# A fixed order for three engines in the scan and attention stage, and the scan's output in five parts

## The chip, the core and the metric

The kernel runs on one core of a Trainium2 chip. The metric is the time of one execution in microseconds (us), lower is better. A core has TensorE (PE, matrix products), VectorE (DVE), ScalarE (ACT) and GpSimd (POOL) for work on whole tiles, and SyncE (SP), which here only issues DMA transfers. Each engine takes its own list of instructions and waits on semaphores where it needs another engine's result or a free buffer. TensorE reads SBUF and writes PSUM, which has eight banks.

## The reference

One encoder layer over a prompt of 256 tokens and a sample of 2048 tokens, 2304 rows of 1024 in all, with float32 accuracy. A normalised input is projected once; the columns split into an RWKV-7 group (eight heads of 64, scanned forward and backward) and an attention group (eight query heads, two key heads). What the change touches:

```python
# scan, for each head, in both directions
S = S * w_t + sa * b_t + v_t * k_t          # 64 x 64 state
y_t = S r_t
y = y_f + y_b
yn = (y - mean(y)) * rsqrt(var(y) + 64e-5)  # over the 64 of a head
out_rwkv = (yn * lnx_w + lnx_b + bonus) * g
# attention, blocks of 128 queries
p = softmax(q k^T / 8);  out_att = p v
```

Both outputs are joined, projected, and followed by a gated feed-forward block.

## The kernel before

The work runs in stages: input projection with the preparation of the scan's operands (`e_phase`) to about 865 us; the start of attention beside the end of that preparation and the first two triangular inversions, to about 1015 us; scan and attention side by side, to about 2425 us; output projection and feed-forward for three groups of 768 rows, to the end.

**Interleaving.** Scan, attention and inversions are Python generators. `beside` runs the scan and for each of its yields calls attention `RATE_S` times the yielded weight (3.45 calls for a weight of 1). One call of attention emits one unit. In the scan's `rest(k)` each element also calls the inversions (`back`) once; it has eight elements in steps 0 to 3 and five in the others, and a step has four rests.

**Scan** (`scan`, `scan_chain`). 36 steps; step `k` takes one 64-token chunk forward and one backward. A step has three dependent parts on TensorE with copies on ScalarE between them (lines 720 to 731), the state update on VectorE (734, 736), and the output sum (742, 745). The Gram matmuls of the next step (`scan_gram`, line 664) and the transposes (`scan_turn`) use PSUM tiles `g`, of which there are two. In the first visit to a chunk its output goes to DRAM (`yd`), in the second it is read back (`y2`) and added (`yt`, line 762). When both chunks of a 128-token tile are done, `scan_out` centres and scales it (lines 780 to 788, with a mean and a power on POOL), transposes it into a `g` tile, multiplies by `g` from DRAM (`yg`, line 805), adds `bg` (`ybg`) on POOL (line 807) and stores it from `yo`. `yo`, `yg` and `ybg` have one buffer each. Tiles become complete in pairs, at every second step of the second half.

**Attention** (`att_scores`, `att_values`). For each group of four heads and each tile of 128 queries there are 16 units (four for a prompt tile): a unit is one head against 512 keys. Scores take two matmuls (lines 934, 935: keys in a high and a low part) into PSUM tile `as` (two banks); VectorE takes the row maximum (938); ScalarE the exponential `p` with its sum (939). After the last unit the factors `f` follow, and POOL multiplies all 16 `p` tiles by them (956). The values run behind, in halves, two per unit: one half transposes four `p` blocks into `at` (968) and splits them into a high part on ScalarE (`pth`, line 177) and a low part on VectorE (`ptl`, line 183); the next half multiplies both with the values (979). `ATT_LAG` sets how many units the values lie behind.

**Order.** A planner orders the instructions of each engine by estimated times and by priority, which goes by the source's order; `high_priority(offset=AHEAD)` moves the maximum, the exponential and the split forward. In the scan and the rest of attention `manual_schedule` fixes TensorE to the order of the source; VectorE, ScalarE, POOL and SP are planned. Outside this stage all are planned.

**Inversions** (`inv_block`). Ten blocks, (group, direction), in a fixed order, four of them (`INV_POOL`) on POOL: load, 31 steps of two operations (lines 570, 572), a transposed copy, stores and loads, a wait of 16 calls, then up to four rounds of matmuls, a masked product (604) and a copy. `load(k + 2)` in the scan calls `back` without a pause until the blocks that the step needs are ready.

The functions that the change touches:

Of the kernel before, what the change touches and what calls it, by code (L numbers as in the profile page):

```python
# [12 lines left out]
ALU = mybir.AluOpType  # L13
# [30 lines left out]
AHEAD = 300  # L44
ATT_LAG = 2
RATE_E, RATE_S = 1.0, 3.45
PB, XB, W_BUFS = 22, 2, 4
# [51 lines left out]
class Kern:  # L99
# [441 lines left out]
    def inv_block(self, bi, d, sb, eng):  # L541
# [25 lines left out]
        yield  # L567
# [7 lines left out]
        nc.vector.tensor_copy(out=xt, in_=xs.rearrange(tr))  # L575
# [18 lines left out]
        for _ in range(16):  # L594
            yield
# [106 lines left out]
    def scan_chain(self, step, nxt, sb, ps):  # L702
# [25 lines left out]
        act.copy(out=sg[0:64, :, 1, :], in_=hb[64:128].rearrange(f))  # L728
        yield
# [14 lines left out]
        for d, q, e, rows in heads:  # L744
            nc.tensor.matmul(psy[rows, d, q, :], mrb[:, d, q, e, :], sav[0:64, d, q, e, :], start=False, stop=d + q == 4,
                             skip_group_check=True)
        if nxt is not None:
            self.scan_sv(nxt, st, sb)
# [5 lines left out]
        else:  # L754
            for d, c in enumerate(step["c"]):
                y2 = T("y2", [P, 4, C], 2)
                self.ld(y2, self.yd[c])
# [4 lines left out]
                dve.tensor_tensor(out=yt[:, c % 2], in0=psy[:, d], in1=y2, op=ALU.add)  # L762
                self.ydone[tile] = self.ydone.get(tile, 0) + 1
                if self.ydone[tile] == 2:
                    self.outs.append(self.scan_out(tile, yt, sb, ps))
                    next(self.outs[-1])
        yield

    def scan_out(self, tile, y, sb, ps):
# [18 lines left out]
        dve.tensor_tensor(out=hv, in0=hv, in1=bc(r), op=ALU.mult)  # L788
        yield
# [4 lines left out]

        g = T("yg", [P, 2, 2, P], 1)
        bg = T("ybg", [P, 2, 2, P], 1)
        yo = T("yo", [P, 2, 2, P], 1)
        half = lambda t, q: t[q % 2 * 64:q % 2 * 64 + 64, q // 2]
        dr = lambda t, t0=t0: t.rearrange("(e c) t -> c e t", e=2)[:, :, t0:t0 + P]
        for q in range(4):  # L800
            self.ld(half(g, q), dr(self.gdr[q]))
            self.ld(half(bg, q), dr(self.bgd[q]))
# [8 lines left out]
    def scan(self, back, sb, ps):  # L811
# [31 lines left out]
        for k, step in enumerate(steps):  # L843
            last = k + 1 == len(steps)
            chain = self.scan_chain(step, None if last or steps[k + 1]["st"] is not step["st"] else steps[k + 1], sb, ps)
            for d in range(2):
# [3 lines left out]
                for i, r in enumerate(rest(k)):  # L850
                    if d == 0 and i == 2:

                        for g in self.outs:
                            next(g, None)
                        self.outs = []
                    yield r
            next(chain)
            yield from rest(k)
# [4 lines left out]
        for g in self.outs:  # L863
            next(g, None)


    def att_kv(self, g, sb, ps):
# [5 lines left out]
        def load(b):  # L873
            if b < len(KBLOCKS):
# [4 lines left out]
                for i in range(2):  # L879
                    self.lda(kd[:, :w, i, :], self.kd[t0:t1, gs].rearrange("(j p) c -> p j c", p=P))  # L880
                self.lda(vr, self.vd[t0:t1, gs].rearrange("(j p) c -> p j c", p=P))
# [18 lines left out]
    def att_q(self, g, t0, sb, ps):  # L900
# [3 lines left out]
        for i in range(2):  # L904
            self.lda(qd[:, :, i, :], self.qd[t0:t0 + P, g * 256:(g + 1) * 256].rearrange("p (h c) -> p h c", c=64))
# [10 lines left out]
    def att_scores(self, qs, t0, kv, sb, ps):  # L916
# [13 lines left out]
        for i in range(nh):  # L930
            kh, kl = kv[parts[i]][:2]
            for h in range(4):
                pss = ps.tile([P, 512], F32, name="as", tag="as", bufs=2)
                nc.tensor.matmul(pss[:, :hw], qs[:, h, :], kh, start=True, stop=False)  # L934
                nc.tensor.matmul(pss[:, :hw], qs[:, h, :], kl, start=False, stop=True)  # L935
                p_ = S("p", [P, 512], PB)
                with self.tc.high_priority(offset=AHEAD):
                    dve.tensor_reduce(out=nm[:, h, i:i + 1], in_=pss[:, :hw], axis=AX.X, op=ALU.max, negate=True)  # L938
                    act.activation(out=p_[:, :hw], in_=pss[:, :hw], func=AF.Exp, bias=nm[:, h, i:i + 1],  # L939
                                   accum_out=ls[:, h, i:i + 1])  # L940
                pt[h, i] = p_
                yield
# [555 lines left out]
```

## Time and profile before

| | |
|---|---|
| time, median of 3 runs | 4222.75 us (4220.28 to 4224.4) |
| the profiled execution | 4225.85 us, span of its instructions 4224.1 us |
| busy, share of the span | PE 91%, DVE 67%, ACT 48%, POOL 32% |
| chain that ended last | PE 65%, DVE 15%, POOL 6%, issue 5%, DMA 4%, ACT 3% |
| mean granted TensorE clock | 0.953 of 2.4 GHz |

The profile is one execution. Engines are busy while they execute; matmuls are pipelined and their ends are modelled, so a busy PE is not PE at its peak. PEld is TensorE's loading of the stationary operand, SPq and ACTq are the DMA issues of an engine. A row `A <- B: us, times` says how long engine and line A sat idle until B released it.

### The profile page before, as it was taken

How to read it: one execution, taken by the hardware profiler on the slowest of the kernel's cores; microseconds unless marked ns; L12 is line 12 of the kernel's file. 1: busy time of each engine (PE TensorE's matmuls, PEld its weight loads, DVE VectorE, ACT ScalarE, POOL GpSimd, SP SyncE). 2: the span in 40 equal slices, each digit the busy share in tenths (PEclk: the TensorE clock that was granted, in tenths of full speed). 3: DMA queues.
4: the chain of work that ended last, by engine and by line, in shares of the span. 5: the costliest groups of instructions: out<-in, count | busy, mean ns of one | idle time of the engine just before them, and what ended most of it. 6: DMA issues, size and time to landing. Idle time of an engine off the chain costs nothing.

```text
span 4224.1 us, 70455 instructions
## 1 busy us (share of the span) xinstructions
PE 3846.1 (91%) x26208; PEld 3306.5 (78%) x26208; DVE 2828.8 (67%) x4337; ACT 2041.3 (48%) x3922; POOL 1351.2 (32%) x1882
## 2 busy tenths in 40 slices
PE   8999999878888887887888879999989999989998
PEld 7988878656666665666666669998879998889987
DVE  5477686899776866667776657764477754477743
ACT  5344444456655564556565634443344443344432
POOL 2244353634636362734344312210122210122200
PEclk9999999789989998989999989999999999999999
DMA  6576576652443335333332252324523343423241
GB/s 201 164 211 211 182 207 199 195 137 43 108 90 85 78 75 120 88 80 92 88 90 72 62 181 83 102 95 175 175 93 99 104 171 109 165 88 107 100 170 70
DMA packets 646871, 524.27 MB, mean 124 GB/s; under 512 B 368512, under 2 KB 555520, under 8 KB 646528
## 3 DMA queue, kind: packets, MB, share of 16 engines
q1 hardware_dynamic: 576944, 438.23, 35.0%
q0 software_dynamic: 16944, 68.43, 4.9%
q10 hardware_dynamic: 52640, 13.11, 1.4%
q8 instruction: 206, 3.38, 0.3%
q14 instruction: 137, 1.12, 0.1%
HBM read 355.59 MB, written 166.37 MB: 124 GB/s over the span
## 4 chain that ended last, share of the span: by engine, by line
PE 65%; DVE 15%; POOL 6%; issue 5%; DMA 4%; ACT 3%; SPq 2%; ACTq 0%; DVEq 0%; POOLq 0%
PE acc L1171 22%; PE acc L213 8%; PE acc L214 8%; PE acc L215 8%; PE ao L979 3%; PE at L968 3%; DVE nm L938 3%; DVE ptl L183 2%; PE g L664 2%; PE as L934 2%; DVE cl L668 1%; PE as L935 1%; POOL p L956 1%; SPq L112 1%; DVE i L570 1%
## 5 line engine op out<-in xcount | busy, mean ns | idle before, releaser
L1171 PE MATMUL acc<-H,wsh 128*128 128x384 f32 x3168 | 813.7, 337 | 32.2 <-ACT cg L1199 22.6
L1171 PEld LDWEIGHTS acc<-H,wsh 128*128 128x128 f32 x3168 | 577.6, 190 | 35.8 <-ACT cg L1199 23.8
L1171 PE MATMUL acc<-H,wsl 128*128 128x384 f32 x1584 | 532.5, 336 | 0.0
L939 ACT ACTIVATE p<-as,nm 128x512 f32<-128x512 f32 (+1 forms) x528 | 360.6, 683 | 182.9 <-DVE nm L938 162.4
L213 PE MATMUL acc<-wsh,H 128*128 128x512 f32 x1080 | 421.1, 391 | 23.3 <-ACT wsh L177 22.8
L938 DVE TENSOR_REDUCE nm<-as 128x1 f32<-128x512 f32 (+1 forms) x528 | 356.9, 678 | 116.2 <-PE as L935 109.1
L956 POOL TENSOR_SCALAR p<-p,f 128x512 f32<-128x512 f32 (+1 forms) x528 | 364.0, 720 | 213.2 <-DVE f L952 188.1
L214 PE MATMUL acc<-wsl,H 128*128 128x512 f32 x1080 | 420.3, 389 | 0.0
L215 PE MATMUL acc<-wsh,H 128*128 128x512 f32 x1080 | 415.3, 389 | 0.0
L183 DVE TENSOR_TENSOR ptl<-at,pth 128x512 fp32r<-128x512 f32 x520 | 354.5, 684 | 71.6 <-ACT pth L177 69.1
L177 ACT CAST pth<-at 128x512 fp32r<-128x512 f32 x520 | 301.6, 586 | 177.7 <-PE at L968 169.9
L968 PE MATMUL at<-ident,p 128*128 128x128 f32 x2080 | 341.0, 289 | 22.5 <-POOL p L956 22.2
L213 PE MATMUL acc<-hThi,wih 128*128 128x384 f32 x1008 | 351.8, 349 | 1.1 <-ACT hThi L177 1.1
L214 PE MATMUL acc<-hTlo,wih 128*128 128x384 f32 x1008 | 348.7, 346 | 0.0
L215 PE MATMUL acc<-hThi,wil 128*128 128x384 f32 x1008 | 348.6, 346 | 0.1
L968 PEld LDWEIGHTS at<-ident,p 128*128 128x128 f32 x2080 | 263.6, 148 | 84.9 <-POOL p L956 34.2
L177 ACT CAST wsh<-wsr 128x1024 fp32r<-128x1024 f32 x156 | 164.2, 1052 | 306.3 <-PE acc L1171 152.2
L183 DVE TENSOR_TENSOR wsl<-wsr,wsh 128x1024 fp32r<-128x1024 f32 x156 | 190.9, 1224 | 175.6 <-ACT wsh L177 175.4
L1171 PEld LDWEIGHTS acc<-H,wsl 128*128 128x128 f32 x1584 | 300.2, 190 | 0.0
L934 PE MATMUL as<-kh,qs 128*128 128x512 f32 (+1 forms) x528 | 264.0, 500 | 34.7 <-ACT p L939 24.7
L979 PE MATMUL ao<-ptl,vst 128*128 128x512 f32 x520 | 234.3, 451 | 61.9 <-DVE ptl L183 60.4
L1114 POOL TENSOR_TENSOR sw<-wsr 128x512 f32<-128x512 f32 x66 | 89.2, 1352 | 621.7 <-DVE wsl L183 551.2
(665 smaller groups left out, 8255.3 us busy)
## 6 DMA issues: line engine op xcount, KB each, us to landing
wsr<-in_ffn_gate SPq DMA_DIRECT2D x66, 512.0 KB, 3.5
wsr<-in_ffn_up SPq DMA_DIRECT2D x66, 512.0 KB, 3.8
wsr<-in_ffn_down SPq DMA_DIRECT2D x66, 512.0 KB, 3.5
wir<-in_w_in POOLq DMA_DIRECT2D x63, 512.0 KB, 4.6
hd<-hid POOLq DMA_DIRECT2D x66, 384.0 KB, 3.6
H<-hd SPq DMA_DIRECT2D x33, 768.0 KB, 6.0
cl<-ard SPq DMA_DIRECT2D x144, 128.0 KB, 3.0
zT<-z SPq DMA_DIRECT2D x84, 192.0 KB, 2.7
```

Of the source, the lines that this page charges most:

```text
L177: nc.scalar.copy(out=hi, in_=src)
L183: e.tensor_tensor(out=lo, in0=src, in1=hi.bitcast(F32), op=ALU.subtract)
L213: mm(out, ahi, bhi, start=first, stop=False)
L214: mm(out, ahi, blo, start=False, stop=False)
L215: mm(out, alo, bhi, start=False, stop=last)
L934: nc.tensor.matmul(pss[:, :hw], qs[:, h, :], kh, start=True, stop=False)
L938: dve.tensor_reduce(out=nm[:, h, i:i + 1], in_=pss[:, :hw], axis=AX.X, op=ALU.max, negate=True)
L939: act.activation(out=p_[:, :hw], in_=pss[:, :hw], func=AF.Exp, bias=nm[:, h, i:i + 1], accum_out=ls[:, h, i:i + 1])
L956: pool.tensor_scalar(out=t, in0=t, scalar1=f[:, h, i:i + 1], scalar2=1.0, op0=ALU.mult, op1=ALU.mult)
L968: nc.tensor.transpose(tp[:, h, :], pt[h, i][:, k * P:(k + 1) * P], self.ident)
L979: nc.tensor.matmul(pso, lhs, t, start=n + m == 0, stop=n + m == len(keys))
L1171: nc.tensor.matmul(acc, x[l][:, k, :], y_[r][:, k, :], start=first and k == 0 and i == 0, stop=k == 3 and i == 2, skip_group_check=True)
```

## The change

The order of TensorE, VectorE and ScalarE is fixed to the source's in the scan and in the rest of attention; POOL and SP stay planned. The priorities go. The source's order is rearranged with it:

- A unit emits scores and maximum, then a half of the values, then the scan's piece, another half, and then the exponential. The four VectorE operations on `f` and POOL's multiplications come after unit 1 of the next query tile. `ATT_LAG` is 3.
- `scan_out` has five parts, one at a call of `norms()`: in each rest the elements 0, 1, 3, 4 (and 6, 7) make one call, and tiles go one after the other. The loads of `yg` and `ybg` are in part four, transposes and products in part five. After the last step the remaining parts follow with a weight of 0.2 each.
- The output sum of a step is taken up two elements later; the `y2` loads come a part earlier.
- The inversions wait five calls instead of one after their first loads, and 24 instead of 16 on POOL; a POOL block's transposed copy moves to POOL.
- The loads of keys, values and queries for attention are issued by SP instead of ScalarE.

```diff
-AHEAD = 300
-ATT_LAG = 2
+ATT_LAG = 3
+FIXED = {mybir.EngineType.PE, mybir.EngineType.DVE, mybir.EngineType.Activation}
...
     def inv_block(self, bi, d, sb, eng):
-        yield
+        for _ in range(5):
+            yield
...
-        nc.vector.tensor_copy(out=xt, in_=xs.rearrange(tr))
+        eng.tensor_copy(out=xt, in_=xs.rearrange(tr))
...
-        for _ in range(16):
+        for _ in range(16 if eng is nc.vector else 24):
...
     def scan_chain(self, step, nxt, sb, ps):
+        y2 = []
+        if not first:
+            for c in step["c"]:
+                y2.append(T("y2", [P, 4, C], 2))
+                self.ld(y2[-1], self.yd[c])
         yield
...
+        yield
         if nxt is not None:
             self.scan_sv(nxt, st, sb)
...
-                    next(self.outs[-1])
...
     def scan_out(self, tile, y, sb, ps):
         pool.tensor_scalar(out=s1, in0=s1, scalar1=1.0 / C, scalar2=0.0, op0=ALU.mult, op1=ALU.add)
+        yield
         dve.tensor_tensor(out=hv, in0=hv, in1=bc(s1), op=ALU.subtract)
         sq = T("ysq", [P, 8, C])
         nc.scalar.activation(out=sq, in_=hv, func=AF.Square)
+        yield
         s2 = T("s2", [P, 8], 2)
         dve.tensor_reduce(out=s2, in_=sq, axis=AX.X, op=ALU.add)
         r = self.rstd(sb, s2, 8, 1.0 / C, 64e-5, "r8")
+        yield
         dve.tensor_tensor(out=hv, in0=hv, in1=bc(r), op=ALU.mult)
...
+        yield
+        pst = ps.tile([P, 2, 2, P], F32, name="g", tag="g", bufs=2)
...
     def scan(self, back, sb, ps):
+        def norms():
+
+            while self.outs and next(self.outs[0], self) is self:
+                self.outs.pop(0)
+
         def rest(k):
             n = 8 if k < 4 else 5
             for i in range(n):
                 next(back, None)
                 yield 1 / n
+                if i % 3 != 2:
+                    norms()
...
-            yield from rest(k)
+            for i, r in enumerate(rest(k)):
+                if i == 2:
+                    next(chain)
+                yield r
...
-        for g in self.outs:
-            next(g, None)
+        while self.outs:
+            norms()
+            yield 0.2
...
-            self.lda(qd[:, :, i, :], self.qd[t0:t0 + P, g * 256:(g + 1) * 256].rearrange("p (h c) -> p h c", c=64))
+            self.ld(qd[:, :, i, :], self.qd[t0:t0 + P, g * 256:(g + 1) * 256].rearrange("p (h c) -> p h c", c=64))
...
     def att_scores(self, qs, t0, kv, sb, ps):
+                dve.tensor_reduce(out=nm[:, h, i:i + 1], in_=pss[:, :hw], axis=AX.X, op=ALU.max, negate=True)
+                yield
                 p_ = S("p", [P, 512], PB)
-                with self.tc.high_priority(offset=AHEAD):
-                    dve.tensor_reduce(out=nm[:, h, i:i + 1], in_=pss[:, :hw], axis=AX.X, op=ALU.max, negate=True)
-                    act.activation(out=p_[:, :hw], in_=pss[:, :hw], func=AF.Exp, bias=nm[:, h, i:i + 1],
-                                   accum_out=ls[:, h, i:i + 1])
+                act.activation(out=p_[:, :hw], in_=pss[:, :hw], func=AF.Exp, bias=nm[:, h, i:i + 1],
+                               accum_out=ls[:, h, i:i + 1])
...
         act.activation(out=f, in_=f, func=AF.Exp)
+        self.att_p = (pt, parts, hw // P)
+        yield
         dve.tensor_tensor(out=ls, in0=ls, in1=f, op=ALU.mult)
...
     def attention(self, sb, ps, heads=(0, 1), tiles=ATT_ORDER):
+                for u in range(units):
+                    next(sc)
+                    half()
                     if u in (0, units - 3):
                         next(qg, None)
-                    half()
                     yield
                     half()
+                    if u == 1:
+                        next(norm, None)
+                    next(sc)
+                next(norm, None)
+                norm = sc
...
-                with tc.manual_schedule(engines={mybir.EngineType.PE}):
+                with tc.manual_schedule(engines=FIXED):
                     beside(self.scan(back, sb, ps), RATE_S)
             run(back)
             st_iv.close()
-            with tc.manual_schedule(engines={mybir.EngineType.PE}):
+            with tc.manual_schedule(engines=FIXED):
                 run(att)
```

## Rows read from the trace of the kernel before

**Rows 1.** Windows by stage: us, busy us (and instructions) by engine, granted clock, DMA.
```profile
1015.00:1700.00 685.00, 581.03 (x5600) 457.82 (x5600) 494.36 (x941) 390.85 (x909) 316.77 (x501) 0.91 0.40 91
1700.00:1870.00 170.00, 142.61 (x1316) 113.23 (x1315) 108.36 (x189) 90.01 (x209) 96.85 (x152) 0.86 0.33 81
1870.00:2425.00 555.00, 463.27 (x4700) 364.76 (x4699) 401.94 (x705) 344.88 (x794) 231.17 (x326) 0.94 0.31 81
2425.00:2520.00 95.00, 72.81 (x333) 60.76 (x334) 40.95 (x43) 31.68 (x41) 11.27 (x19) 0.87 0.53 183
```
**Rows 2.** One line's instructions: duration ns, first and last start us.
```profile
L722 ACT COPY ry<-hb x36: 567/586/587, 1030.7 to 2400.9; 128x512 f32<-128x512 f32 x36
```
**Rows 3.** Waits of TensorE, 1015 to 1700 us: us in total, times, longest.
```profile
PE ao L979 <- DVE ptl L183: 27.8, 46, 2.2
PE at L968 <- POOL p L956: 15.4, 20, 7.3
PE as L934 <- ACT p L939: 12.0, 12, 2.2
PE as L934 <- DVE qs L912: 6.6, 3, 4.6
...
PE as L909 <- ACT p L939: 5.4, 5, 2.2
```
**Rows 4.** Waits of TensorE, 1700 to 2425 us.
```profile
PE g L664 <- DVE yo L805: 29.1, 5, 9.6
PE ao L979 <- DVE ptl L183: 28.5, 60, 1.4
PE g L664 <- issue: 27.9, 3, 14.1
PE at L968 <- POOL p L956: 6.1, 13, 2.5
...
PE as L909 <- ACT p L939: 5.3, 6, 1.9
...
PE as L934 <- ACT p L939: 3.7, 7, 0.7
```
**Rows 5.** Timeline, 1202 to 1208 us: start us, us, instruction, idle before.
```profile
1202.97 0.42 DVE L572 TENSOR_TENSOR i<-i,i 128x247 f32<-128x247 f32 x1
...
1203.30 0.39 PE L935 MATMUL as<-kl,qs 128*128 128x512 f32 x1
...
1205.68 0.69 DVE L938 TENSOR_REDUCE nm<-as 128x1 f32<-128x512 f32 x1
...
1207.24 0.66 PE L909 MATMUL as<-ident,qdup 128*128 128x128 f32 x4 [2.18 <-ACT p L939]
```
**Rows 6.** Timeline around one pair of output tiles.
```profile
2007.84 1.26 POOL L807 TENSOR_TENSOR yo<-yo,ybg 128x512 f32<-128x512 f32 x1
2009.12 2.54 SPq L112 DMA_DIRECT2D yT<-yo  x4
...
2013.39 0.76 DVE L805 TENSOR_TENSOR yo<-g,yg 128x256 f32<-128x256 f32 x2 [14.00 <-DMA yT<-yo]
...
2014.24 2.04 PE L664 MATMUL g<-cl,bk__22527 64*128 64x128 f32 x14 [14.10 <-issue]
```
**Rows 7.** Windows of that stall and of the hole behind the stage.
```profile
1999.50:2013.50 14.00, 0.65 (x10) 0.39 (x6) 0.11 (x1) 1.75 (x5) 9.60 (x14) 0.63 0.23 55
...
2424.50:2447.00 22.50, 0.00 (x0) 0.00 (x0) 2.77 (x4) 2.57 (x3) 1.55 (x2) 0.50 0.75 265
```
**Rows 8.** DMA issues, 1700 to 2425 us: KB, median us to landing.
```profile
yg<-gdr SPq DMA_DIRECT2D x67, 64.0 KB, 2.3
yT<-yo SPq DMA_DIRECT2D x64, 64.0 KB, 2.1
```
**Rows 9.** Groups by line, 1015 to 2425 us: busy us, mean ns, idle before.
```profile
L956 POOL TENSOR_SCALAR p<-p,f 128x512 f32<-128x512 f32 (+1 forms) x464 | 316.0, 712 | 131.9 <-DVE f L952 125.8 <-ACT qs L911 5.6
...
L163 POOL TENSOR_TENSOR r<-r,mhalf 128x8 f32<-128x8 f32 x18 | 30.7, 1705 | 1.4
```

More of the change, by code (lines that the diff above doesn't have):

```diff
@@ L761, in scan_chain @@
                 yt = self.yt[tile]
-                dve.tensor_tensor(out=yt[:, c % 2], in0=psy[:, d], in1=y2, op=ALU.add)
+                dve.tensor_tensor(out=yt[:, c % 2], in0=psy[:, d], in1=y2[d], op=ALU.add)
                 self.ydone[tile] = self.ydone.get(tile, 0) + 1
@@ L787, in scan_out @@
         r = self.rstd(sb, s2, 8, 1.0 / C, 64e-5, "r8")
+        yield
         dve.tensor_tensor(out=hv, in0=hv, in1=bc(r), op=ALU.mult)
+        g = T("yg", [P, 2, 2, P], 1)
+        bg = T("ybg", [P, 2, 2, P], 1)
+        half = lambda t, q: t[q % 2 * 64:q % 2 * 64 + 64, q // 2]
+        dr = lambda t, t0=t0: t.rearrange("(e c) t -> c e t", e=2)[:, :, t0:t0 + P]
+        for q in range(4):
+            self.ld(half(g, q), dr(self.gdr[q]))
+            self.ld(half(bg, q), dr(self.bgd[q]))
         yield
@@ L793, in scan_out @@
                 nc.tensor.transpose(pst[:, j, k, :], y[:, k, 2 * j:2 * j + 2, :].rearrange("p q c -> p (q c)"), self.ident)
-        g = T("yg", [P, 2, 2, P], 1)
-        bg = T("ybg", [P, 2, 2, P], 1)
         yo = T("yo", [P, 2, 2, P], 1)
[L798 to L802, printed above, removed]
         for j in range(2):
@@ L849, in scan @@
                     self.scan_gram(steps[k + 1], d, sb, ps)
-                for i, r in enumerate(rest(k)):
-                    if d == 0 and i == 2:
-                        for g in self.outs:
-                            next(g, None)
-                        self.outs = []
-                    yield r
+                yield from rest(k)
             next(chain)
-            yield from rest(k)
+            for i, r in enumerate(rest(k)):
+                if i == 2:
+                    next(chain)
+                yield r
             if not last:
@@ L956, in att_scores @@
                 pool.tensor_scalar(out=t, in0=t, scalar1=f[:, h, i:i + 1], scalar2=1.0, op0=ALU.mult, op1=ALU.mult)
-        self.att_p = (pt, parts, hw // P)
     def att_values(self, g, t0, kv, p, sb, ps, store):
@@ L968, in turned @@
                 nc.tensor.transpose(tp[:, h, :], pt[h, i][:, k * P:(k + 1) * P], self.ident)
-            with self.tc.high_priority(offset=AHEAD):
-                return self.split(sb, tp.rearrange("p h q -> p (h q)"), [P, 512], "pt", bufs=3)
+            return self.split(sb, tp.rearrange("p h q -> p (h q)"), [P, 512], "pt", bufs=3)
         hl = [turned(*keys[0])]
@@ L995, in attention @@
         nc = self.nc
-        pend = []
+        pend, norm = [], iter(())
         def half():
@@ L1017, in attention @@
                 units = 4 if j * P < TP else 16
-                for u, _ in enumerate(self.att_scores(qs, j * P, kv, sb, ps)):
+                sc = self.att_scores(qs, j * P, kv, sb, ps)
+                for u in range(units):
+                    next(sc)
+                    half()
                     if u in (0, units - 3):
                         next(qg, None)
-                    half()
                     yield
                     half()
+                    if u == 1:
+                        next(norm, None)
+                    next(sc)
+                next(norm, None)
+                norm = sc
                 if not pend:
@@ L1028, in attention @@
                 pend.append(self.att_values(g, j * P, kv, self.att_p, sb, ps, nc.scalar if last else nc.sync))
+        next(norm, None)
         while pend:
```

10 lines of the change are left out of this document (3 added, 7 removed).

## The prediction, made before the changed kernel was run

> **What bounds the kernel now.** I read the page first: TensorE is busy 91% of the span, and the chain that ended last is 65% TensorE. That is a mean over unlike stages, so next I cut the span by stage [rows 1]. The change touches 1015 to 2425 us, where scan and attention run side by side (36 scan steps, 39.1 us apart on average: first and last copy `ry`, [rows 2]), and the hole behind it. Three stretches make up these 1410 us. TensorE is busy 581.0, 142.6 and 463.3 us of 685, 170 and 555, so idle 104.0 + 27.4 + 91.7 = 223.1 us; its granted clock averages 0.91, 0.86 and 0.94. Read as a mix of its two levels, 2.4 and 1.2 GHz, that is 2 x (0.09 x 685 + 0.14 x 170 + 0.06 x 555) = 237 us at the lower one; at a busy share of 0.84 it costs about 237 x 0.84 / 2 = 100 us. VectorE is busy 1005 us of the 1410, so no order can bring the stage below about 1000.
>
> Then I asked who ended TensorE's idle time, in both halves [rows 3, 4]. Four causes stand out.
> - Value matmuls (line 979) waiting for the low half `ptl` from VectorE: 27.8 + 28.5 = 56.3 us in 106 waits, so half a microsecond each.
> - Score matmuls and query transposes waiting for a score bank that the exponential still reads: 12.0 + 5.4 + 3.7 + 5.3 = 26.4 us; and 6.6 us for `qs`.
> - The scan's Gram matmuls (line 664), in eight waits only: 29.1 + 27.9 = 57.0 us.
> - Transposes of the normalised scores waiting for POOL: 15.4 + 6.1 = 21.5 us.
>
> **What the planner's order does.** In [rows 5] the scores end at 1203.7 us, yet their maximum starts at 1205.68: VectorE ran inverse and Gram work first. The exponential follows, and the next transposes start after 2.18 us of idle TensorE. In [rows 6] two output tiles meet: the second tile's product (line 805) waits 14.00 us on VectorE until the first tile's `yo` is stored, because `yo` has one buffer and POOL's add for it stood behind a burst of normalisations. Only then does a Gram bank come free: TensorE waits 14.10 us. In those 14 us TensorE works 0.65 us and VectorE 0.11, at a mean clock of 0.63 (the first of [rows 7]). There are eight such pairs of tiles (and a ninth at the end), which is the 57.0 us.
>
> **The change, part by part.**
>
> *1. Fixed order of VectorE, `ptl`.* A turned block is used two units after its transposes, and between the two TensorE has at least two score pairs, a value pair and four transposes, while ScalarE's cast and VectorE's subtraction are two operations on 512 columns, like the 0.69 us of the maximum in [rows 5]. The subtraction now always comes right behind one maximum. 56.3 us to between 0 and 56.3 (if VectorE's load, not its order, is the cause); nearer to the rows of order, [rows 5]: I take 18. **-38**.
>
> *2. Fixed order, score banks and `qs`.* The maximum stands directly behind the scores, the exponential half a unit later, behind one cast; the bank is wanted again a unit after that. 26.4 + 6.6 = 33.0 us to between 0 and 33.0; I take 13: **-20**.
>
> *3. Output in five parts.* The `yg` and `ybg` loads move a part ahead of their use, and B's last part comes five calls after A's last. A rest has five elements (39.1 / 20 = 2.0 us each) with calls in four, so that is some 12 us, against 1.3 (add) + 2.5 (stores) + 2.1 (landing) = 6 us with a free POOL [rows 6, 8]. So the wait for A's store goes unless a burst falls in it. What is late next: the loads. Eight issues at 0.63 us and 2.3 us of landing [rows 6, 8] are 7.3 us, against one or two elements, about 2.4, between parts four and five: some 4.9 us of VectorE for 16 tiles, 78 us. TensorE can run ahead by what its two score banks allow, so I charge it 40%: 31. Bounds 5 and 78. From 57.0 to about 30: **-27**.
>
> *4. Normalisation later, lag 3.* POOL's 16 multiplications of a query tile start after the next tile's unit 1 instead of at its start; the values start one unit later. The room before the first transposes shrinks by about one unit, but the four small VectorE operations ahead of POOL now run together. 21.5 us to between 10 and 45; I take 25: **+3**.
>
> *5. New handoffs to POOL in a fixed order.* POOL is still planned. Each of 18 tiles sends a mean and an `r` there, 36 handoffs, and VectorE takes each up at the next call, 2.0 us later. POOL is in normalisation bursts 316 of 1410 us (22%), a burst is 16 x 0.71 = 11.4 us [rows 9], so a handoff that meets one waits 5.7 - 2.0 = 3.7 us on average: 36 x 0.22 x 3.7 = 30; `r` itself takes 1.7 us and uses up its distance, some 7 more. Of these 37 us of VectorE 40% reach TensorE: **+15**. Bounds 0 (all hidden) and 36 x 2.5 = 90.
>
> *6. Inversions take more calls* (4 more for the delay of their loads, 8 more on POOL). Blocks three to eight now need 3 x 62 + 3 x 70 = 396 calls when the loads of step 18 want them; 4 x 32 + 12 x 20 + 15 = 383 have been made. 13 calls then run in one go, once: four rounds of matmuls, product, matmuls and copy, each with three dependent operations of up to 0.69 us; bounds 0 and 9, **+5**.
>
> *7. The tail.* From 2424.5 to 2447 TensorE does nothing (the second of [rows 7]): the last two output tiles finish, then the output projection's loads are issued and split. Now the second tile starts its five parts after the first has finished: five operations on 512 columns and `r`, 5 x 0.69 + 1.7 = 5.2 us, and its loads 5 more. By the calls, attention still runs out a few units before the scan ends (needs 2 more, has made 4 more before 1015 us), so nothing covers it. Bounds 0 and 20: **+10**.
>
> *8. The clock.* If idle time falls by a quarter, I give back a quarter of the 100 us: **-25**, bounds 0 and 60.
>
> At nothing: `y2` loads issued earlier; the moved `qdup`, `kdup` and `vr` loads, which leave ScalarE's queue for SP's and line up behind the scan's loads there at 0.6 us an issue. The queries' cover is some 13 units between load and use; without it each would cost its landing. `kdup` has one buffer and no cover, before as after.
>
> Sum: -38 - 20 - 27 + 3 + 15 + 5 + 10 - 25 = -77 us. The profiled execution took 4225.85 us (span 4224.1), 3 us over the median 4222.75; 4225.85 - 77 = **4149 us**.
>
> **Rivals.**
>
> *A, slower: VectorE's queue is blocked by POOL.* In fixed order a subtraction or product that waits for POOL or for a load holds up every maximum behind it, and with those the exponentials, the score banks and TensorE. Such a block stands in [rows 6], its price in [rows 7]: 14 us in which almost nothing runs. The planner places `r`'s use where its estimate has `r` ready; the source fixes it one call later, whatever POOL does. If each of the 36 handoffs costs TensorE 2.5 us, the output pairs stay at 57.0 and the clock gives nothing back, the sum is -38 - 20 + 3 + 90 + 5 + 10 = +50: 4276 us. It decides from 92 / 36 = 2.6 us a handoff on, if all other terms stand. Against it: bursts fill only 22% of the time. The Trainium skill ("PSUM — Partial Sum Buffer", "Engine vs sequencer instructions") has this as a rule: "ScalarE/VectorE/GpSimdE queues are strict FIFO". The trace agrees: VectorE starts nothing in the 14.00 us. By that rule alone, every wait that is written into the order is paid in full by VectorE; what the page doesn't say is how much TensorE feels.
>
> *B, no change: load, not order.* With inversions VectorE has two operations of up to 0.42 us beside the maximum and the subtraction of 0.69 [rows 5] in many units, so it may be the bound there; then 1 and 2 give little, 3 is eaten by 5, and the time stays near 4220.
>
> *C, much faster.* If the half-microsecond waits vanish everywhere, idle falls by 163 to some 60 us, half of the clock's 100 comes back, and the tail costs 10: 4225.85 - 163 - 50 + 10 = 4023 us.
>
> **Chances.** Forecast 0.60 (its own range 4075 to 4215), A 0.20, B 0.08, C 0.12. 0.2% (8 us) is about what a measurement of this kernel can tell from no change. Faster 0.60 + 0.12 = 0.72, the same 0.08, slower 0.20. The range runs from C's time, of which the lower part is left out, to part of A: 4030 to 4245.
>
> **What would show it.** In the scan stage `ptl` waits under 25 us and score-bank waits under 20; Gram waits behind line 805 under 35 us with none over 8; VectorE idle ahead of lines 782, 788 and 805 shows POOL and `yg` by name; the hole before the output projection about 32 us; steps near 37 us. A mean step over 39 us, with VectorE waiting for `r` or `yg` for over 100 us, is A. The projection before 865 us and the feed-forward stage after should be unchanged to a few us; if they moved, the planner's other choices moved, and the sum is wrong for a reason outside it.

## The result, and the profile after

The changed kernel takes 4396.68 us (median of 4 runs, 4394.41 to 4399.2) against 4221.62: ratio 1.0414, 95% interval 1.0396 to 1.0432. It is slower by 175 us, where 4149 us were forecast; the range (4030 to 4245) does not hold it.

The profiled execution has a span of 4393.7 us, 169.6 more than before. Two views place the loss. The first is the group of the first copy of each scan step, which answers to [rows 2]:

```profile
L723 ACT COPY ry<-hb x36: 567/585/588, 1048.2 to 2568.7; 128x512 f32<-128x512 f32 x36
```

First to last copy took 1370.2 us; now it is 1520.5: +150.3, or 43.4 us a step instead of 39.1. The first copy comes 17.5 us later. The stretch from the last copy to the output projection's first matmul is 45.7 us instead of 46.3, and all that follows is 2.4 us longer. The second view is the windows that answer to [rows 1], cut at the first, 17th and last copy (us; busy us and instructions of PE, PEld, DVE, ACT, POOL; clock; DMA). Before:

```profile
1030.70:1671.90 641.20, 545.99 (x5258) 430.74 (x5258) 462.92 (x878) 364.61 (x848) 301.69 (x478) 0.91 0.39 89
1671.90:2400.90 729.00, 610.00 (x6041) 481.39 (x6042) 512.65 (x899) 442.37 (x1029) 334.37 (x488) 0.92 0.33 85
```

After:

```profile
1048.20:1736.50 688.30, 555.37 (x5170) 430.86 (x5170) 448.33 (x818) 356.00 (x835) 304.94 (x479) 0.90 0.35 81
1736.50:2568.70 832.20, 660.56 (x6111) 512.48 (x6112) 536.99 (x964) 439.61 (x1029) 338.84 (x491) 0.89 0.30 77
```

TensorE was busy for 1156.0 us in these steps (11,299 matmul records) and is now for 1215.9 (11,281). So the +150.3 are 90.4 us more idle TensorE (214.2 to 304.6) and 59.9 us more busy time for the same work, at a granted clock of 0.90 and 0.89 instead of 0.91 and 0.92. Both halves lose, the first too, in which no output part runs. VectorE and ScalarE are busy about as long as before (985 us instead of 976, 796 instead of 807): this is order, not load.

What TensorE waited for from the first to the last copy (answers to [rows 3, 4]), before:

```profile
PE ao L979 <- DVE ptl L183: 52.7, 101, 2.2
PE g L664 <- issue: 30.8, 4, 14.1
PE g L664 <- DVE yo L805: 29.1, 5, 9.6
PE at L968 <- POOL p L956: 21.5, 33, 7.3
PE as L934 <- ACT p L939: 15.6, 19, 2.2
PE as L909 <- ACT p L939: 10.6, 11, 2.2
PE as L934 <- DVE qs L912: 8.8, 5, 4.6
```

After:

```profile
PE as L946 <- ACT p L951: 115.1, 113, 4.2
PE ao L992 <- DVE ptl L183: 43.7, 41, 10.8
PE at L982 <- POOL p L971: 26.9, 62, 3.8
PE ao L992 <- ACT pth L177: 21.1, 10, 10.7
PE as L905 <- DMA kdup<-kd: 18.2, 3, 8.1
PE as L946 <- DVE qs L924: 17.6, 16, 2.7
PE as L921 <- ACT p L951: 16.2, 26, 1.6
...
PE g L808 <- DVE yt L795: 10.1, 6, 2.3
...
PE g L665 <- issue: 3.2, 1, 3.2
```

Score banks and `qs` went from 35.0 to 115.1 + 16.2 + 17.6 = 148.9 us, `ptl` from 52.7 to 43.7, Gram and output transposes from 59.9 to 13.3, `p` from POOL from 21.5 to 26.9, `pth` from 7.1 to 21.1, `kdup` from 6.5 to 18.2. The differences, +113.9 - 9.0 - 46.6 + 5.4 + 14.0 + 11.7 = +89.4, account for the 90.4 us of idle time. One row is by far the largest: scores wait for an exponential that has not yet left their bank. And what VectorE, then ScalarE, waited for meanwhile:

```profile
DVE ptl L183 <- ACT pth L177: 230.6, 225, 6.3
DVE cl L669 <- PE g L665: 93.5, 62, 5.6
DVE yt L795 <- POOL r L163: 39.9, 14, 10.2
...
DVE yt L787 <- POOL s L785: 21.6, 9, 10.0
```
```profile
ACT pth L177 <- PE at L982: 252.8, 178, 11.9
ACT p L951 <- DVE nm L948: 104.4, 121, 4.6
ACT mr L672 <- DVE cl L669: 95.5, 124, 5.4
ACT xo L611 <- PE g L610: 61.4, 30, 5.7
ACT ysq L789 <- DVE yt L787: 60.1, 16, 11.8
```

Read them as a ring: the exponential stands behind a cast that waits for TensorE's transposes; the maximum behind a subtraction that waits for that cast; TensorE's scores behind the exponential.

Few of these waits name POOL, but three of them are long, and TensorE's share in them is filed under `ptl` and `pth`. VectorE waits 10.00, 10.19 and 10.11 us for a mean or an `r` that stands behind POOL's 16 multiplications of a query tile (10.7 to 11.1 us); the subtraction or the cast behind it is late, and TensorE waits 10.73, 10.82 and 8.74 us for the value matmuls' operand. The second of the three:

```profile
2135.14 0.69 DVE L795 TENSOR_TENSOR yt<-yt,r 128x512 f32<-128x512 f32 x1 [10.19 <-POOL r L163]
...
2136.49 0.80 PE L992 MATMUL ao<-ptl,vst 128*128 128x512 f32 x1 [10.82 <-DVE ptl L183]
```

So 30.3 us of TensorE's idle time in the second half are rival A's mechanism. What is left of `ptl` and `pth` is 34.5 us, against 59.8 before.

How the ring looks in time, with the main instructions of three units of the changed kernel (start us, duration, instruction, idle before):

```profile
1314.34 0.50 PE L946 MATMUL as<-kh,qs 128*128 128x512 f32 x1 [0.48 <-ACT p L951]
...
1314.66 0.68 DVE L948 TENSOR_REDUCE nm<-as 128x1 f32<-128x512 f32 x1
...
1315.43 0.69 ACT L951 ACTIVATE p<-as,nm 128x512 f32<-128x512 f32 x1 [0.67 <-DVE nm L948]
...
1316.60 0.48 PE L946 MATMUL as<-kh,qs 128*128 128x512 f32 x1
1316.60 0.68 DVE L183 TENSOR_TENSOR ptl<-at,pth 128x512 fp32r<-128x512 f32 x1
...
1317.20 0.68 DVE L948 TENSOR_REDUCE nm<-as 128x1 f32<-128x512 f32 x1
...
1317.97 0.69 ACT L951 ACTIVATE p<-as,nm 128x512 f32<-128x512 f32 x1 [0.31 <-DVE nm L948]
...
1318.80 0.50 PE L946 MATMUL as<-kh,qs 128*128 128x512 f32 x1 [0.53 <-ACT p L951]
```

The scores of 1314.34 have their maximum at 1317.20, because VectorE is still at the unit before (the maximum at 1314.66 is that unit's), then at four inversion steps left out here, and then at the subtraction of 1316.60; it does not wait in this stretch. Their exponential runs at 1317.97; and the scores two units on, which need the bank, wait until 1318.80. Two units take 4.46 us. Pairing the n-th score, maximum and exponential of the trace over the first 16 steps gives 2.12 us from the start of a score to its maximum and 2.10 from there to the exponential. With TensorE alone fixed (the first run below) it is 1.21 and 0.83.

What filled these gaps can be added up from the trace over all 447 units of the steps. From the end of the scores to the start of their maximum it is 614 us (215 with TensorE alone fixed). In them VectorE runs subtractions for 239 us, runs inversion steps for 94, waits for a subtraction's cast for 80 and for POOL for 50. From the end of the maximum to the exponential it is 650 us (75 with TensorE alone fixed): ScalarE runs casts for 128 and waits for their transposes for 134, but it also waits for scan work, for VectorE's Gram product (`mr`) 88, for `xo` 42 and for the centred tile (`ysq`) 42. So the cast and the subtraction are the largest part of what stands ahead, in good part by their own running time, and not all of it.

### The profile page after: what moved, and what is told of

The parts are those of the page before. It is cut to its first block, busy times and chain, and to the rows that moved or that the text cites. A ratio compares the mean times of both kernels' runs of the same rounds, so it can differ in the third digit from the quotient of the medians.

```text
span 4393.7 us, 70454 instructions
## 1 busy us (share of the span) xinstructions
PE 3916.2 (89%) x26208; PEld 3347.7 (76%) x26208; DVE 2839.4 (65%) x4333; ACT 2031.2 (46%) x3922; POOL 1355.4 (31%) x1886
## 4 chain that ended last, share of the span: by engine, by line
PE 63%; DVE 15%; POOL 8%; ACT 5%; issue 5%; DMA 3%; SPq 1%; ACTq 0%; POOLq 0%; DVEq 0%
PE acc L1193 21%; PE acc L213 8%; PE acc L214 8%; PE acc L215 8%; PE ao L992 3%; PE at L982 2%; DVE ptl L183 2%; PE as L946 2%; POOL p L971 2%; DVE nm L948 2%; PE g L665 2%; DVE cl L669 2%; ACT p L951 1%; POOL i L573 1%; PE as L947 1%
## 5 line engine op out<-in xcount | busy, mean ns | idle before, releaser
L213 PE MATMUL acc<-wsh,H 128*128 128x512 f32 x1080 | 421.2, 391 | 15.6 <-ACT wsh L177 14.9
L946 PE MATMUL as<-kh,qs 128*128 128x512 f32 (+1 forms) x528 | 274.7, 520 | 147.1 <-ACT p L951 125.5
L982 PE MATMUL at<-ident,p 128*128 128x128 f32 x2080 | 352.4, 293 | 27.7 <-POOL p L971 27.3
L982 PEld LDWEIGHTS at<-ident,p 128*128 128x128 f32 x2080 | 267.5, 150 | 100.0 <-POOL p L971 46.3
L1136 POOL TENSOR_TENSOR sw<-wsr 128x512 f32<-128x512 f32 x66 | 89.1, 1350 | 623.0 <-DVE wsl L183 551.9
L946 PEld LDWEIGHTS as<-kh,qs 128*128 128x128 f32 x528 | 108.0, 204 | 221.0 <-ACT p L951 190.1
```

The source lines that it names most:

```text
L213: mm(out, ahi, bhi, start=first, stop=False)
L982: nc.tensor.transpose(tp[:, h, :], pt[h, i][:, k * P:(k + 1) * P], self.ident)
```

## The experiments

Sixteen kernels ran on the chip beside before, whose median was between 4222.6 and 4229.2 us in each set. "16" and "19" are the us from the first to the 17th and from there to the last `ry` in the profiled execution. These columns come from one execution each: the first 16 steps of the two runs with TensorE alone fixed, with and without hand-offs to POOL, have the same source and differ by 14 us (627.4 and 613.0).

| run | median us | ratio, 95% interval | 16 | 19 |
|---|---|---|---|---|
| before | 4221.62 | 1 | 641.2 | 729.0 |
| after | 4396.68 | 1.0414 (1.0396 to 1.0432) | 688.3 | 832.2 |
| TensorE alone fixed | 4188.21 | 0.9897 (0.987 to 0.9925) | 627.4 | 702.5 |
| TensorE, VectorE fixed | 4319.58 | 1.0221 (1.0196 to 1.0246) | 675.7 | 787.9 |
| TensorE, ScalarE fixed | 4307.29 | 1.0183 (1.0158 to 1.0208) | 662.2 | 770.3 |
| before's source, all three fixed | 4710.59 | 1.1142 (1.1119 to 1.1165) | 793.8 | 1035.0 |
| split one half later | 4366.67 | 1.0339 (1.0323 to 1.0354) | 689.7 | 812.0 |
| three more calls for POOL | 4351.92 | 1.0305 (1.0287 to 1.0322) | 695.9 | 786.6 |
| before with the five parts alone | 4181.97 | 0.9894 (0.9878 to 0.991) | 642.2 | 680.4 |
| Gram copies later | 4376.88 | 1.0361 (1.0345 to 1.0376) | 688.4 | 820.3 |
| all scan consumers later | 4545.64 | 1.0746 (1.0719 to 1.0773) | 765.0 | 906.8 |
| the same with all room | 4454.09 | 1.0534 (1.0509 to 1.0559) | 755.1 | 821.2 |
| no inversion steps, all fixed | 4324.8 | 1.0238 (1.0221 to 1.0255) | 652.6 | 818.1 |
| the same, TensorE alone | 4134.72 | 0.9787 (0.9763 to 0.9811) | 590.8 | 678.9 |
| no hand-offs to POOL, all fixed | 4335.69 | 1.0265 (1.0241 to 1.0289) | 689.3 | 778.5 |
| the same, TensorE alone | 4173.8 | 0.9877 (0.9853 to 0.9901) | 613.0 | 681.5 |
| subtraction alone later | 4354.96 | 1.0314 (1.0294 to 1.0334) | 668.9 | 811.3 |
| the same, exponential earlier | 4382.64 | 1.038 (1.0358 to 1.0402) | 689.2 | 819.0 |

### Which engine's fixed order

Four kernels: three are the changed one with fewer engines in `FIXED`, the fourth is before with all three.

```diff
-FIXED = {PE, DVE, Activation}
+FIXED = {PE}                 # first; then {PE, DVE}; then {PE, Activation}
-    with tc.manual_schedule(engines={mybir.EngineType.PE}):
+    with tc.manual_schedule(engines=FIXED):     # the fourth, in before, all three
```

> The changed source, with TensorE alone in fixed order (as before); everything else of the change stays. S, ScalarE's fixed order (exponentials held behind copies that wait): about 4220 us. V, VectorE's fixed order (POOL handoffs): about 4220 us. R, the rearranged source itself (exponential a half unit later, five output parts, lag 3): stays near 4390 us.

> The changed source, TensorE and VectorE fixed, ScalarE planned. S: most of the loss of 175 us is gone, about 4250 us, and TensorE's waits for a score bank fall from 133 us to under 50. V: near 4390 us, with VectorE's waits for POOL (67 us) as they are. R: near 4390 us.

> The changed source, TensorE and ScalarE fixed, VectorE planned. V: about 4250 us, the waits for POOL gone. S: near 4390 us, score-bank waits still over 100 us. R: near 4390 us.

> The kernel before with nothing changed but the order: TensorE, VectorE and ScalarE fixed to its own source order. S and V: slower than before, 4350 us or more, since its output parts and inversions leave no room between an operation and its use. R: about 4220 us.

With TensorE alone fixed the changed kernel is 1% faster than before: rearranged source, moved loads and five parts are together a gain, and the whole loss, 208 us, is the fixed order of the other two. VectorE's alone costs 131 us (4319.58 - 4188.21), ScalarE's alone 119, both 208: less than their sum, so they lose partly the same time. The expectations had put the loss on one engine or the other (about 4250 us with the right one freed, near 4390 with the wrong one); both runs fall between. In the first 16 steps each engine's order makes its own link late: with VectorE's fixed it is 2.18 us from score to maximum and 0.89 to the exponential, with ScalarE's 1.13 and 2.72. Before's source with all three fixed takes 4710.59 us: the rearrangement suits a fixed order (by 314 us), but not well enough. TensorE's waits with it alone fixed, over the steps:

```profile
PE ao L992 <- DVE ptl L183: 72.9, 119, 3.6
PE as L905 <- DMA kdup<-kd: 17.7, 4, 7.8
PE ao L992 <- ACT pth L177: 15.3, 18, 2.7
PE as L946 <- ACT p L951: 13.2, 19, 1.9
```

The planner leaves `ptl` late, as before, and has the maximum and the exponential as early as before (1.20 and 0.83 us there): it gives way on the half-microsecond waits that the prediction wanted to remove, and gets the score banks for it.

### The five output parts alone

Before, with the diff's hunks on `scan_chain`, `scan_out` and `scan`; nothing of the attention, `FIXED` or the inversions.

> The kernel before, TensorE alone fixed, with only the scan's output in five parts, the earlier load of y2 and the later output sum; attention as before. If the gain of the rearranged source with planned VectorE and ScalarE (41 us) is that of the output parts: about 4180 us, with the Gram waits behind the output product (57 us) gone. If it is that of the attention unit: about 4220 us.

Its expectation, about 4180 us, came. With TensorE alone fixed above (4188.21), from which it cannot be told apart, it is the fastest of the kernels that do the whole work. The 19 steps shrink from 729.0 to 680.4, the 16 are as before, and TensorE's waits in the 19 show why:

```profile
PE g L664 <- issue: 7.0, 4, 3.4
PE g L807 <- DVE yt L794: 5.7, 1, 5.7
```

The Gram waits of [rows 4], 57.0 us, are 7.0 and 5.7.

### Distance for the split, for POOL and for the Gram copies

Each of these is the changed kernel with one thing moved; all three engines stay fixed.

```diff
             for h in range(4):
                 nc.tensor.transpose(...)
-            return self.split(...)
+            return tp                   # split written one half later
```
```diff
         pool.tensor_scalar(out=s1, ...)
         yield
+        yield
...
         r = self.rstd(...)
         yield
+        yield
+        yield
```
```diff
-            nc.scalar.copy(out=mr, in_=psg[0:64, :, 64:128])
-            nc.gpsimd.tensor_tensor(out=mrb[:, d, :, e, :], in0=mr, ...)
+        self.late.append(late)          # both, one attention unit later
```

> The changed kernel, all three engines fixed, but a turned block's cast and subtraction are written one half later, behind the next unit's scores and maximum, so that neither queue stands behind transposes that have only just been issued. U, the unit itself (in the changed order VectorE waits 244 us and ScalarE 261 us for fresh transposes, and the next maximum and exponential stand behind): 4300 us or less, score-bank waits under 70 us. P, the handoffs to POOL: stays within 25 us of 4397. M, the Gram copies that wait on ScalarE for VectorE's product: within 25 us of 4397.

> The changed kernel with one more call between the mean's handoff to POOL and its use, and two more between the handoff of r and its use (eight calls an output tile instead of five). P: VectorE's 67 us of waits for POOL nearly vanish, and with them the 25 us of TensorE in front of the output's transposes; 4340 to 4360 us. U or M: 4380 us or more.

> The changed kernel with the Gram copies on ScalarE (and POOL's product of them) written one attention unit after VectorE's products of the same banks. M: the 97 us that ScalarE waits for those products go, the exponentials behind them come earlier, 4340 us or less. U or P: within 25 us of 4397.

They regain 30, 45 and 20 us. The 19 steps are 20, 46 and 12 us shorter; the first 16 are not shorter in any. For the hand-offs to POOL the expected time (4340 to 4360) came; for the split (4300 or less) and the Gram copies (4340 or less) it did not. Over the steps VectorE's waits for `pth` fell from 230.6 to 92.8 us with the late split, and ScalarE's behind the Gram products from 95.5 to 29.9 in the last; the time did not follow, and TensorE's waits for `ptl` rose from 43.7 to 89.1 us with the late split and to 58.6 in the last. None of the three is the whole cause; the room for POOL is worth about a fifth of the 208 us.

### All consumers of the scan later

If these stood at the head of the queues while TensorE was still at their matmuls, writing them a unit later had to help. The edit is the same for `cl`, `mr`, the state's copies and update, `am` and `xo`.

```diff
-        act.copy(out=ry, in_=hb)
+        self.later(lambda: act.copy(out=ry, in_=hb))
...
```

> The changed kernel, with all VectorE and ScalarE work that takes the scan's and the inversions' products from PSUM (Gram products, `ry`, state copies and update, masked product, `xo`) written one attention unit after the matmuls instead of right behind them. Theory Q (in the fixed order these stand at the head of the queues while TensorE is still at the matmuls, and hold the maxima and exponentials behind them, in both halves of the stage): at least 60 us come back, 4335 us or less, the first 16 steps fall from 688 us to under 665, and ScalarE's waits for the Gram product fall from 97 us to under 35. Rival N (the loss does not come from the scan's consumers): within 25 us of the run that delayed the Gram copies alone (4377), first 16 steps still over 680.

> The run before together with the two other distances: the cast and subtraction of a turned block one half later, and three more calls between GpSimd's results and their use. All three engines are still fixed to the source. If the loss is only missing distance between a product and its use (Q and the two theories before it, adding up: at least 60 + 30 + 45), the time comes to 4260 us or less, and near 4190 if nothing is left. If a fixed order costs by itself, because no distance is right for durations that change with the clock and with the inversions, it stays over 4300 although every wait named so far is gone or smaller.

Of the first run neither number came: it is 169 us slower than with the Gram copies alone moved. With both other distances added it is still 57 us over the changed kernel; over 4300 was the sign for a fixed order that costs by itself, but the condition beside it, that every named wait shrinks, was not met: ScalarE waits 99.8 us for the Gram products there. The first edit did not even remove the waits that it was meant for: ScalarE still waits 91.6 us for the Gram products. So it says that this distance is no cure, and not that the theory is wrong. In the first 16 steps the units of attention with a piece of scan in them last 4.99 us instead of 4.32. That the delays lengthen the scan's own chain is the obvious reading, but it is not shown: TensorE's waits for the chain's tile `hb` stay at 5.4 us, and those that grew are for the score banks (115.1 to 145.9) and the masked product `am` (12.1 to 31.6).

### Inversions, and the hand-offs to POOL

Two pairs, each with all three fixed and with TensorE alone. The first pair leaves out the 31 inversion steps on VectorE, the second the mean's division and the power on POOL.

```diff
         for j in range(31):
-            eng.tensor_tensor(...)
-            eng.tensor_tensor(...)
+            if eng is not nc.vector:
+                ...
...
-        pool.tensor_scalar(out=s1, ...)
-        r = self.rstd(sb, s2, 8, 1.0 / C, 64e-5, "r8")
-        dve.tensor_tensor(out=hv, in0=hv, in1=bc(r), op=ALU.mult)
+        dve.tensor_tensor(out=hv, in0=hv, in1=bc(s2), op=ALU.mult)
```

> The changed kernel without the 31 steps of two VectorE operations in each inversion that VectorE does (their calls are still made; the inversions on GpSimd are left as they are). All three engines fixed. It is compared with the next run, in which only TensorE is fixed; with the steps, that pair differs by 688.3 - 627.4 = 61 us in the first 16 scan steps and by 832.2 - 702.5 = 130 in the other 19. Theory F (the steps need nothing of TensorE; a planner puts them where VectorE would idle, the source puts a pair of them ahead of every maximum): without them the difference in the first 16 steps falls below 25 us. Rival H (it is the loop of attention itself, score to maximum to exponential to score bank, run through queues that also hold casts and subtractions waiting for TensorE): it stays at 45 us or more. Both expect no change of the difference in the other 19 steps, where few inversions are left.

> As the run before, with TensorE alone fixed. F and H: faster than the 4188 us of the run with the steps, since VectorE has some 100 us less to do; its own time tells nothing apart, its difference to the run before does.

> The changed kernel with the normalisation of the scan's output handed to GpSimd nowhere: the division of the mean and the power are left out (the output is scaled by the plain sums), so VectorE's five operations follow each other without a wait for GpSimd. All three engines fixed. Compared with the next run (TensorE alone fixed) in the last 19 steps, where the full pair differs by 130 us. If the waits for GpSimd are what the fixed order loses in that half (rival A of the prediction), the difference falls below 50 us. If they are only what three more calls regained (45 us), it stays at 75 us or more, and the rest is the same loop as in the first half. Both: no change in the first 16 steps (61).

> As the run before, with TensorE alone fixed. Within 10 us of 4188: the planned order hides the hand-offs to GpSimd already.

In the 16 steps fixing the two engines costs 652.6 - 590.8 = 61.8 us without the inversions' steps and 60.9 with them, so these are not it (rival H's 45 us or more came). (The POOL pair gives 689.3 - 613.0 = 76.3 there, where no change from 61 was expected: that is the spread of one execution. By the medians the cost is 190 us without the inversions' steps, 208 with them.) In the 19 steps it costs 778.5 - 681.5 = 97.0 without hand-offs to POOL, 129.7 with them: a quarter of that half's loss, 33 us, is waiting for POOL and most of it is not (75 us or more was the sign for that), about the 30.3 us of the three long waits. By the medians it is 208 - 162 = 47 us, as much as the room for POOL regained. The last kernel is outside its expectation, 14 us under the 4188 instead of at most 10.

What is left has the same shape in both halves. TensorE's timeline, cut at each first score matmul (line 946), tells which units of attention grew. In the first 16 steps, 123 units without scan or inversion matmuls last 1.91 us on average with TensorE alone fixed and 2.39 with all three; 70 units with a piece of scan in them last 4.37 and 4.32 us (the one long stretch without scores, 83 and 89 us, is left out). 123 x 0.48 = 59 us is nearly all of that half's 60.9. In the other 19 it is 160 units x (2.44 - 1.90) = 86 and 91 units x (4.53 - 4.12) = 37, together 123 of the 130. There it is not all the ring: the long waits for POOL lie in these units too.

### Two links of the ring

```diff
-            return self.split(...)      # cast and subtraction
+            act.copy(out=hi, in_=tp)    # the cast in place,
+            return tp, hi               # the subtraction one half later
```
```diff
                     yield
+                    next(sc)            # the exponential
                     half()              # transposes and cast
-                    next(sc)
```

> The changed kernel with VectorE's subtraction of a turned block (line 183) alone written one half later, so behind the next unit's maximum; ScalarE's cast stays. The units of attention without a piece of the scan between their scores and the next last 2.40 us in the changed kernel and 1.90 with TensorE alone fixed (first 16 steps). Theory L1 (VectorE's link: the maximum stands behind a subtraction that waits for the cast): such units fall to 2.15 us or less, the first 16 steps to 655 us or less, the time below 4330. Theory L2 (ScalarE's link: the exponential stands behind a cast that waits for the transposes): units stay over 2.3 us, the first 16 steps over 675.

> As the run before, and the exponential written ahead of its unit's second half, so ahead of the cast that waits for the transposes. L2: units without scan fall to 2.15 us or less, the first 16 steps to 655 us or less, the time below 4330. L1: no gain over the run before beyond 15 us. If neither order of the source shortens those units (a third case: any fixed place is late once the scan has delayed one engine), units stay over 2.3 us in both.

| first 16 steps | score to maximum | maximum to exponential | units without scan | with scan |
|---|---|---|---|---|
| TensorE alone fixed | 1.21 | 0.83 | 1.91 | 4.37 |
| TensorE, VectorE fixed | 2.18 | 0.89 | 2.17 | 4.57 |
| TensorE, ScalarE fixed | 1.13 | 2.72 | 2.24 | 4.22 |
| after | 2.12 | 2.10 | 2.39 | 4.32 |
| split later | 1.55 | 1.82 | 2.20 | 4.60 |
| subtraction later | 1.43 | 2.48 | 2.27 | 4.20 |
| and exponential earlier | 1.52 | 1.73 | 2.22 | 4.60 |

Neither theory's number came: 668.9 and 689.2 us for the 16 steps, 2.27 and 2.22 for the units. Each link does what it was said to do, in part. With the subtraction out of its way the maximum comes 0.7 us earlier, but the exponential, still behind the cast, gives back 0.4 of it; with both out of the way the ring is shorter by 0.97 us, and the units that carry scan are longer by 0.28, while TensorE's waits for `ptl` and `pth` over the steps went from 64.8 to 125.0 us: now the cast and the subtraction are late for the value matmuls. What still stands ahead of the exponential then is mostly scan work on ScalarE: of 495 us between maximum and exponential it waits 92 for the Gram product, 56 for `xo` and 45 for `ysq`. That is nearest to the third case of the expectation, though its number (over 2.3 us) is missed as well. TensorE's waits with the subtraction alone later:

```profile
PE as L946 <- ACT p L951: 106.4, 85, 3.7
PE ao L1002 <- DVE ptl L990: 70.9, 66, 10.9
```

The score banks' 115.1 became 106.4 and `ptl`'s 43.7 became 70.9.

## Why the prediction was wrong, step by step

*1, `ptl`.* 18 us forecast, 43.7 found. Two waits of 10.82 and 8.74 us in it are VectorE's blocks for POOL, which belong to step 5; without hand-offs to POOL this wait is 15.6 us, near the forecast.

*2, score banks and `qs`.* This is the step that failed: 33.0 us were to become 13 and became 148.9. "The maximum stands directly behind the scores" is true of the list. In time it stands behind what is ahead of it in VectorE's queue: inversion steps, and a subtraction that may itself wait for ScalarE's cast, which waits for transposes of the unit before. The exponential, "behind one cast" in the prediction, stands behind that cast and behind scan copies that wait too. The bound of 0 to 33.0 left a loss out altogether: it took the planner's lateness, [rows 5], for the whole cost of an order, and did not ask what the planner gained by taking instructions out of turn. The runs price that: 131 us for VectorE's order, 119 for ScalarE's, 208 for both.

*3, five parts.* Right in its size, and the largest gain: 57.0 us were to become 30; they are 13.3 in the steps and two output transposes of 8.0 and 7.5 us after the last (2589.83 and 2598.40 us). Done alone the parts shorten the kernel by 1.06%. The wait that came next was for POOL's `r`, not for the loads, so the size came by another way than the prediction's.

*4, normalisation.* 25 forecast, 26.9 found.

*5, hand-offs to POOL.* 15 us with bounds of 0 and 90; by the pairs without POOL it is 33 us (47 by the medians). The mechanism is the one foreseen, a hand-off that meets a burst; but three met one almost whole, where 3.7 us was the mean wait, and in these TensorE felt all of VectorE's 30.3 us, not 40%.

*6, the inversions' burst,* 5 us, was not told apart from the rest.

*7, the tail.* +10 forecast, -0.6 found (45.7 us from the last `ry` to the projection instead of 46.3). The hole itself is 14.95 us instead of 22.85; 15.4 us of waiting for the two transposes above, instead of 4.3, take up the difference.

*8, the clock.* 25 us were to come back. As idle time rose, TensorE's busy time for the same work rose by 59.9 us: nothing came back, as the idle time of step 2 went the other way.

*Left out.* The `kdup` loads behind SP's other issues: priced at nothing, 18.2 us of waiting against 6.5; that the queue is the reason was not tried by itself, but the run of the five parts alone, which leaves them to ScalarE, has 3.5, and TensorE alone fixed, which moves them, 17.7. And the first step starts 17.5 us later, with TensorE alone fixed too (1047.8 us), so the fixed order of the others is not needed for it; with the five parts alone it starts at 1033.4. The cause stays open.

*Rival A* had the right sign and the smaller mechanism: the three long waits are it. Steps are over 39 us, but VectorE waits 61.5 us for POOL's mean and `r`, not over 100, and taking POOL away leaves 97 of 130 us in the second half and nothing to explain the first. The page that it leaned on, of the Trainium skill ("PSUM — Partial Sum Buffer", "Engine vs sequencer instructions"), calls the queues strict FIFO. The runs agree: VectorE starts nothing in the 10.19 us for `r`, though the casts for the two subtractions behind it end 9.55 us earlier. They show what that page does not: the dearest head of such a queue was no wait for POOL but the subtraction, 239 us of running and 80 of waiting for its cast ahead of maxima whose scores were done, against 50 for POOL.

*Open.* No order of the source that was tried brings the ring near the planner's 1.21 and 0.83 us; that none exists is not shown. Nor is it shown how many score banks it would take to hide the ring, since the stage's tiles (`as`, `at` and `g` twice, `ao`, `hb`) use all eight PSUM banks.

## What to carry to other kernels

An order fixed for one engine is a plan; the same source order fixed for three engines that feed each other in a ring made each wait for the others here. Before fixing it, follow one unit round the ring, and for every operation ask what stands ahead of it and what that waits for: "directly behind in the source" is no time. And run the parts of a bundled change by themselves: here one part gained 1.06% and another cost 5% of the time.

## What the runs showed of the hardware

Lost time on TensorE came with more than its idle time. From TensorE alone fixed to all three fixed, the same matmuls (11,286 and 11,281 records in the steps) went from 1153.97 to 1215.9 us busy, so 62 us on top of 129 us more idle time. With TensorE alone fixed the windows are:

```profile
1047.80:1675.20 627.40, 541.11 (x5175) 433.69 (x5177) 433.98 (x798) 358.23 (x837) 306.15 (x479) 0.89 0.39 90
1675.20:2377.70 702.50, 612.86 (x6111) 484.49 (x6108) 543.01 (x964) 442.08 (x1029) 339.85 (x491) 0.95 0.35 90
```

In the second half the granted clock fell from 0.95 to 0.89 and busy time rose by 48 us. In the first it went from 0.89 to 0.90 and busy time still rose by 14 us, so the clock is not all of it; what the rest is was not tried. With all scan consumers later the matmuls are busy for 1298.94 us at granted clocks of 0.83 and 0.85.

There is no fixed price. From TensorE alone fixed to that run, each us more of idle TensorE came with (1298.94 - 1153.97) / (372.86 - 175.93) = 0.74 us of slower matmuls, where idle time is the length of the steps less the busy time; to the changed kernel it is 62 / 129 = 0.48. And the two runs with one engine freed are idle for nearly the same time, 251.6 and 258.6 us, and busy for 1212.0 and 1174.0.
